# Mixer weights' low halves on GpSimd, merged reciprocals, paired first outputs of the feed-forward stages, and shifted filling, in a two-layer hybrid encoder on one core

## The chip, the cores and the metric

The kernel runs on one core of a Trainium2 chip. The metric is device time in microseconds (us) of one execution. Five engines matter: TensorE (PE; PEld is its weight load, which overlaps PE), VectorE (DVE), ScalarE (ACT), GpSimd (POOL) and SyncE (SP), which here issues the DMAs.

## The reference

```python
for layer in range(DEPTH):                       # DEPTH = 2, D_MODEL = 1024, SEQ = 512
    xn = rms_norm(h, norm_mix_g[layer])
    if layer % 2 == 0:
        mix = even_mixer(...)   # A: top-128 sparse attention by an indexer, 8 heads; B: chunked attention with a bias, 8 heads
    else:
        mix = odd_mixer(...)    # C: forgetting attention, 8 heads; D: sliding window with sinks, 8 query and 2 key heads
    h = h + mix
    h = h + conv_gated_ffn(rms_norm(h, norm_ffn_g[layer]), ...)
return rms_norm(h, norm_out_g)

def conv_gated_ffn(x, w_up, conv_w, conv_b, w_down):      # D_FF = 2816
    g, u = jnp.split(causal_conv3(x @ w_up) + conv_b, 2, axis=-1)
    return (jax.nn.silu(g) * u) @ w_down
```

In A, the indexer's scores are summed over 4 heads, and each query keeps its 128 best admissible keys. Each mixer has an input projection, two groups of heads and an output projection. All numbers are float32.

## The kernel before, in words

**Products.** A float32 product is made of three matmuls on halves: an operand is split into a high half (`hi`, rounded to the matmul's format) and a low half (`lo = x - hi`), and `mm3` (lines 176 to 178) issues hi*hi, hi*lo and lo*hi into one PSUM tile. A step of the filling (below) is one such triple of 512 columns.

**Weights.** All weights stream through the class `Stream` in the fixed order `PLAN`, in tiles of 512 KB: SP loads `raw` (2 buffers), ACT makes `whi` (line 136), and line 138 makes `wlo` by a subtraction. The engine of that subtraction is DVE, and POOL for the keys `A1` and `kB` alone (8 tiles). Keys name the stage: `i` and `d` are small projections, `vB`, `qB`, `kB`, `A1`, `vA`, `A2`, `oA`, `oB` belong to layer 0's mixer, `vC`, `qC`, `kC`, `qD`, `oC`, `oD` to layer 1's, and `g`, `u`, `w` to the feed-forward stages.

**Stages.** Layer 0 runs its indexer and its top-k, B, A and the output projection; then come the feed-forward stage, layer 1 with C, D and its projection, and the second feed-forward stage. Two heads make a `Pair`. Its scores go to PSUM, `soft` (lines 436 to 443) makes a softmax for the four row blocks 1, 2, 0, 3 of 256, 384, 128 and 512 columns: a fused add and minimum on DVE (L439), exp with a sum on ACT (L441), a reciprocal on DVE (L442), a scaling on POOL (L443). `turn` transposes P on PE (L453) and splits it by `PTh` (ACT, L183) and `PTl` (DVE, L184); `av` (L470, L471) multiplies by V; `store` writes Y, and with the pair's second head splits it into `yT`.

**Filling.** `weave` puts the softmax of one pair between the turns of the pair before, and in the gaps has PE do steps of other projections: `fill.step`. How many steps each pair's round gets stands in `FILL_B`, `FILL_A`, `FILL_C` and `FILL_D` (lines 77 to 80). Results of a projection leave PSUM by L546 (`os`, DVE), L547 (`qk` high, ACT) and L548 (`qk` low, POOL). PSUM has 2 buffers `acc`, 4 `s` and 2 `tp`.

**Top-k.** For A, three row blocks of width 256, 384 and 512 (tiles `wk_491`, `wk_545` and `wk_611` in the lists of instructions) each go through 16 rounds of MAX8 (L664) and MATCH_REPLACE8 (L665) on DVE, while B runs.

**Order.** The order of instructions on an engine is made by a scheduler when the program is built; PE stays near program order, while DVE, ACT and POOL are reordered. Each engine then works its own list strictly in that order.

**Other names.** `forget_row` builds for each pair of C a tile `sel` on DVE (L921), with which PE spreads one row of F over 128 partitions (L924). `token_roots` and `roots` make the reciprocal norms of the feed-forward input; `up` runs one chain of a feed-forward product.

Of the kernel before, what the change touches and what calls it, by code (L numbers as in the profile page):

```python
# [10 lines left out]
F32 = mybir.dt.float32  # L11
F32R = mybir.dt.float32r
AF = mybir.ActivationFunctionType
OP = mybir.AluOpType
# [59 lines left out]
WIDE_AT = {k: i for i, k in enumerate(WIDE)}  # L74
NI = 324
ND = 264
FILL_B = (8, 20, 21, 22, 22)
FILL_A = (23, 30, 16, 14, 11)
FILL_C = (6, 18, 16, 15, 12)
FILL_D = (10, 9, 9, 9, 8)  # L80
PARTS = (0, 20, 40, 50, 60, 72, 90, 100)
# [5 lines left out]
def trunk(ctx, tc, a, out):  # L87
# [11 lines left out]
    def bank(tag, shape=(128, 512)):  # L99
        return psum.tile(list(shape), F32, name=tag, tag=tag, bufs=banks[tag])  # L100
# [17 lines left out]
    class Stream:  # L118
# [4 lines left out]
        def issue(self):  # L123
            key = PLAN[self.pos]
            self.pos += 1
            if key[0] == "i":
                src, w = a["w_i"][key[1]], 2 * NI
            elif key[0] == "d":
                src, w = a["w_d"][key[1]], 2 * ND
            else:  # L130
                src, w = a["w"][WIDE_AT[key]], 1024
            raw = wp.tile([128, 1024], F32, name="raw", tag="raw", bufs=2)
            nc.sync.dma_start(raw[:, :w], src)
            hi = wp.tile([128, 1024], F32R, name="whi", tag="whi")
            lo = wp.tile([128, 1024], F32R, name="wlo", tag="wlo")
            nc.scalar.activation(hi[:, :w], raw[:, :w], AF.Copy)  # L136
            eng = nc.gpsimd if key[0] in ('A1', 'kB') else nc.vector
            eng.tensor_tensor(lo[:, :w], raw[:, :w], hi[:, :w].bitcast(F32), OP.subtract)  # L138
            self.ready[key] = (hi, lo)

# [41 lines left out]
    def hilo(dh, dl, src):  # L182
        nc.scalar.activation(dh, src, AF.Copy)  # L183
        nc.vector.tensor_tensor(dl, src, dh.bitcast(F32), OP.subtract)  # L184
# [51 lines left out]
    def token_roots():  # L236
        pt = bank("tp", (128, NT))
        for t in range(NT):
            nc.tensor.matmul(pt[:, t:t + 1], hold_ss["t"][:, t * 128:(t + 1) * 128], ones[:, 0:1],
                             start=True, stop=True)  # L240
        inv_root(rs, pt)

    def roots(t0=0, t1=NT, copy=True):
        n = t1 - t0
        dg = sp.tile([128, NT, 128], F32, name="os", tag="os", bufs=1)
        nc.vector.tensor_tensor(dg[:, :n], ident[:, None, :].to_broadcast([128, n, 128]),
                                rs[:, t0:t1][:, :, None].to_broadcast([128, n, 128]), OP.mult)
        pr = bank("tp", (128, NT, 128))
        nc.tensor.matmul(pr[:, :n], ones, dg[:, :n], start=True, stop=True)
        if copy:  # L250
            nc.scalar.activation(R[:, t0 * 128:t1 * 128].rearrange("p (a d) -> p a d", a=n), pr[:, :n], AF.Copy)
        return pr.rearrange("p a d -> p (a d)")
# [6 lines left out]
    class Fill:  # L259
# [15 lines left out]
        def run(self):  # L275
            while self.q:
                self.step(1)
# [35 lines left out]
    def chan_mm(o, ws, c0=0, c1=SEQ):  # L313
        wh, wl = ws
        for k in range(KD):
            mm3(o[:, c0:c1], wh[:, k, :], wl[:, k, :], xT[0][:, k, c0:c1], xT[1][:, k, c0:c1],
                k == 0, k == KD - 1)
            yield
        later.tick()
# [73 lines left out]
    class Pair:  # L393
# [40 lines left out]
            self.L[e][0], self.L[e][2], self.L[e][3] = P[:, 0:128], P[:, 128:512], P[:, 512:1024]  # L434

        def soft(self, e, rows):
            for i in rows:
                L, nm, sm = self.L[e][i], self.nm[e][:, i:i + 1], self.sm[e][:, i:i + 1]
                nc.vector.tensor_tensor_reduce(out=L, in0=self.s[e][i], in1=self.job["bias"][e][i], scale=1.0,  # L439
                                               scalar=3e38, op0=OP.add, op1=OP.min, accum_out=nm)  # L440
                nc.scalar.activation(L, L, AF.Exp, scale=-1.0, bias=nm, accum_out=sm)  # L441
                nc.vector.reciprocal(sm, sm)  # L442
                nc.gpsimd.tensor_scalar(L, L, sm, 1.0, op0=OP.mult, op1=OP.mult)  # L443

        def turn(self, e, n):
            pk = ([0], [1, 3], [2])[n]
# [26 lines left out]
        def store(self, e):  # L473
            job, o = self.job, self.o[e]
            if e == 0:
                job["Y"] = self.mp.tile([128, 512], F32, name="Y", tag="Y", bufs=self.ybufs)
            Y = job["Y"]
            r = slice(64 * e, 64 * e + 64)
            nc.scalar.activation(Y[r], o[64 * (1 - e):64 * (1 - e) + 64], AF.Copy)
            nc.vector.tensor_tensor(Y[r], o[r], Y[r], OP.add)  # L480
            if e == 1:
                y = job["pair"]["y"] = self.mp.tile([128, 2, 512], F32R, name="yT", tag="yT",
                                                    bufs=5 if self.ybufs == 2 else 4)
                hilo(y[:, 0], y[:, 1], Y)

    def weave(prev, cur, fill, n, mid=None, share=PARTS):
        cut = [n * p // 100 for p in share]
# [264 lines left out]
    def ffn(layer, after):  # L752
        with ExitStack() as st:
            fp = st.enter_context(tc.tile_pool(name=f"ffn{layer}", bufs=1))
            cw = fp.tile([128, 192], F32, name="cw")[:, :4 * NC_FF].rearrange("p (a b) -> p a b", b=4)
            nc.sync.dma_start(cw, a["conv"][layer])
            act = [fp.tile([128, 2, SEQ], F32R, name=f"act{j}") for j in range(NFF)]

            def conv(o, c, dst):
                v = fp.tile([128, SEQ], F32, name="ov", tag="ov", bufs=2)  # L760
                nc.vector.tensor_tensor(v, o, R, OP.mult)  # L761
                nc.scalar.activation(dst, v, AF.Identity, scale=cw[:, c, 2:3], bias=cw[:, c, 3:4])
                nc.vector.scalar_tensor_tensor(dst[:, 1:], v[:, :SEQ - 1], cw[:, c, 1:2], dst[:, 1:],
                                               op0=OP.mult, op1=OP.add)
                nc.vector.scalar_tensor_tensor(dst[:, 2:], v[:, :SEQ - 2], cw[:, c, 0:1], dst[:, 2:],
                                               op0=OP.mult, op1=OP.add)

            def up(key):
                W.ahead(2)
                ws = W.get(key, 128)  # L770
                o = bank("acc" if key[0] == "g" else "s")
                run(chan_mm(o, ws))
                return o

            for j in range(NFF):
                tmp = sp.tile([128, 2, SEQ], F32, name="scr", tag="scr")
                g = up(("g", layer, j))
                if j == 0:
                    token_roots()
                    roots()  # L780
                conv(g, j, tmp[:, 0])
                nc.scalar.activation(tmp[:, 0], tmp[:, 0], AF.Silu)
                u = up(("u", layer, j))
                conv(u, NFF + j, tmp[:, 1])
                nc.vector.tensor_tensor(tmp[:, 0], tmp[:, 0], tmp[:, 1], OP.mult)  # L785
                hilo(act[j][:, 0], act[j][:, 1], tmp[:, 0])
            hold = [None]

            def weights(c, k):
                n = c * NFF + k  # L790
                if n % 8 == 0:
                    W.ahead(2)
                    hold[0] = W.get(("w", layer, n // 8), 128)
                return [x[:, n % 8, :] for x in hold[0]]

            for c in range(KD - 1 if layer else KD):
                o = bank("acc")
                for k in range(NFF):
                    wh, wl = weights(c, k)
                    mm3(o, wh, wl, act[k][:, 0], act[k][:, 1], k == 0, k == NFF - 1)  # L800
                add_resid(c, o)
                after(c, slice(0, SEQ))
            if layer:
                ws = [weights(KD - 1, k) for k in range(NFF)]
                for cols in (slice(0, 256), slice(256, 512)):
                    o = bank("acc")
                    lead_sums(cols)
                    for k in range(NFF):
                        mm3(o[:, cols], *ws[k], act[k][:, 0, cols], act[k][:, 1, cols], k == 0, k == NFF - 1)
                    add_resid(KD - 1, o, cols)  # L810
                    after(KD - 1, cols)
# [33 lines left out]
    with ExitStack() as st:  # L845
# [70 lines left out]

        pairs = [{} for _ in range(4)]

        def forget_row(hh, w):
            sel = mp.tile([128, 128], F32R, name="sel", tag="PSh", bufs=1)  # L920
            nc.vector.tensor_tensor(sel, ident[:, hh:hh + 1].to_broadcast([128, 128]),  # L921
                                    ident[:, 32 + hh:33 + hh].to_broadcast([128, 128]), OP.add)
            pb = bank("s")
            nc.tensor.matmul(pb[:, :w], sel, FTh[:, :w], start=True, stop=True)  # L924
            return pb

        def bias_c(bias, hh, pb, rows):
# [292 lines left out]
```

## Time and profile before

| what | value |
|---|---|
| time, median of 3 runs | 1246.18 us (1245.75 to 1247.45) |
| the profiled execution's own time | 1248.47 us |
| its span, first to last instruction | 1246.6 us |
| mean granted TensorE clock | 0.992 |
| PE busy | 1211.3 us, 97% of the span |
| DVE, ACT, POOL busy | 826.8, 592.6, 198.4 us |

The median is a time of whole executions; the profile is one execution, 2.29 us above that median, of which the span covers all but 1.9 us. Busy shares are means over stages: layer 0's mixer takes the first 300 us or so, its feed-forward stage lasts until about 660 us, layer 1's mixer until about 880 us, and the second feed-forward stage fills the rest.

### The profile page before, as it was taken

The page shows a single profiled execution, that of the slowest core. Times are in us where ns is not written, and L with a number is a line of the kernel's source. Part 1 is how long each engine was busy: PE and PEld are TensorE (multiplying, and loading weights), DVE is VectorE, ACT ScalarE, POOL GpSimd, SP SyncE. Part 2 cuts the span into 40 slices and gives each one's busy share as a digit, 9 for nine tenths or more (in the row PEclk, how much of TensorE's full clock was granted, in tenths as well). Part 3 has the DMA queues.
Part 4 walks back from the last instruction along what each step waited for, and adds up shares of the span by engine and source line. Part 5 has one row for each costly group of instructions (what it writes and reads, how often), then busy time and mean ns, then how long its engine had stood idle before and what let it go on. Part 6 is the DMA issues. An engine that isn't in the chain of part 4 may idle for free.

```text
span 1246.6 us, 15944 instructions
## 1 busy us (share of the span) xinstructions
PE 1211.3 (97%) x5908; PEld 996.3 (80%) x5908; DVE 826.8 (66%) x1528; ACT 592.6 (48%) x1008; POOL 198.4 (16%) x275
## 2 busy tenths in 40 slices
PE   8997999999999999999999999999999999999997
PEld 8776788787888888888888877777888888888886
DVE  7999867867777777742325466897777777772222
ACT  6444465656444444432224577785544444442221
POOL 3465322212000000000002254322000000000000
PEclk9998999999999999999999999999999999999999
DMA  6232124312333333333322321122233233223321
GB/s 215 82 105 68 35 68 135 103 50 88 102 101 96 91 100 102 92 95 101 101 64 90 102 68 35 35 76 75 90 102 98 90 100 102 92 95 101 101 68 68
DMA packets 35373, 111.71 MB, mean 90 GB/s; under 512 B 4192, under 2 KB 6624, under 8 KB 35296
## 3 DMA queue, kind: packets, MB, share of 16 engines
q1 hardware_dynamic: 35296, 110.70, 28.5%
q8 instruction: 46, 0.75, 0.3%
q14 instruction: 31, 0.25, 0.1%
HBM read 108.59 MB, written 2.10 MB: 89 GB/s over the span
## 4 chain that ended last, share of the span: by engine, by line
PE 78%; DVE 11%; ACT 5%; issue 3%; DMA 2%; POOL 1%; POOLq 0%; SPq 0%; DVEq 0%; ACTq 0%
PE acc L176 17%; PE acc L177 17%; PE acc L178 17%; PE s L176 7%; PE s L178 7%; PE s L177 7%; DVE wlo L138 2%; DVE wk L665 2%; DVE m L664 2%; PE tp L453 2%; ACT whi L136 1%; ACT P L441 1%; DMA raw<-in_w 1%; DVE xT L231 1%; DVE P L439 1%
## 5 line engine op out<-in xcount | busy, mean ns | idle before, releaser
L138 DVE TENSOR_TENSOR wlo<-raw,whi 128x1024 fp32r<-128x1024 f32 (+2 forms) x188 | 237.1, 1261 | 158.4 <-ACT whi L136 156.1
L136 ACT ACTIVATE whi<-raw 128x1024 fp32r<-128x1024 f32 (+2 forms) x196 | 204.6, 1044 | 210.8 <-PE acc L177 139.4
L176 PE MATMUL acc<-xT,whi 128*128 128x512 f32 x480 | 189.4, 395 | 1.0 <-DVE os L546 0.6
L178 PE MATMUL acc<-xT,wlo 128*128 128x512 f32 x480 | 187.7, 391 | 0.0
L177 PE MATMUL acc<-xT,whi 128*128 128x512 f32 x480 | 187.7, 391 | 0.0
L213 POOL TENSOR_TENSOR scr<-scr,os 128x512 f32<-128x512 f32 x24 | 34.1, 1421 | 730.5 <-ACT os L211 730.5
L176 PE MATMUL acc<-act,whi 128*128 128x512 f32 (+1 forms) x374 | 140.9, 377 | 0.0
L178 PE MATMUL acc<-act,wlo 128*128 128x512 f32 (+1 forms) x374 | 140.9, 377 | 0.0
L177 PE MATMUL acc<-act,whi 128*128 128x512 f32 (+1 forms) x374 | 140.9, 377 | 0.0
L176 PE MATMUL s<-xT,whi 128*128 128x512 f32 x352 | 137.6, 391 | 0.0
L178 PE MATMUL s<-xT,wlo 128*128 128x512 f32 x352 | 137.5, 391 | 0.0
L177 PE MATMUL s<-xT,whi 128*128 128x512 f32 x352 | 137.0, 389 | 0.0
L176 PEld LDWEIGHTS acc<-xT,whi 128*128 128x128 f32 x480 | 90.7, 189 | 20.9 <-issue 1.9
L178 PEld LDWEIGHTS acc<-xT,wlo 128*128 128x128 f32 x480 | 90.6, 189 | 19.1
L177 PEld LDWEIGHTS acc<-xT,whi 128*128 128x128 f32 x480 | 90.6, 189 | 18.0
L176 PE MATMUL acc<-whi,xT 128*128 128x512 f32 (+2 forms) x208 | 84.1, 406 | 2.1 <-ACT whi L136 1.9
L761 DVE TENSOR_TENSOR ov<-s,R 128x512 f32<-128x512 f32 x44 | 30.4, 692 | 79.6 <-PE s L178 79.6
L183 ACT ACTIVATE act<-scr 128x512 fp32r<-128x512 f32 x44 | 27.8, 631 | 115.8 <-DVE scr L785 115.8
L177 PE MATMUL acc<-wlo,xT 128*128 128x512 f32 (+2 forms) x208 | 80.7, 389 | 1.2 <-DVE wlo L138 1.1
L178 PE MATMUL acc<-whi,xT 128*128 128x512 f32 (+2 forms) x208 | 81.0, 390 | 0.1
L177 PEld LDWEIGHTS acc<-act,whi 128*128 128x128 f32 x374 | 70.4, 188 | 13.0
L178 PEld LDWEIGHTS acc<-act,wlo 128*128 128x128 f32 x374 | 70.4, 188 | 12.9
(250 smaller groups left out, 2235.3 us busy)
## 6 DMA issues: line engine op xcount, KB each, us to landing
raw<-in_w SPq DMA_DIRECT2D x188, 512.0 KB, 3.5
h<-in_x SPq DMA_DIRECT2D x16, 256.0 KB, 4.9
T<-in_relb SPq DMA_DIRECT2D x8, 256.0 KB, 3.0
raw<-in_w_i SPq DMA_DIRECT2D x4, 324.0 KB, 4.1
raw<-in_w_d SPq DMA_DIRECT2D x4, 264.0 KB, 2.7
out_y<-h SPq DMA_DIRECT2D x4, 256.0 KB, 2.2
out_y<-h SPq DMA_DIRECT2D x2, 384.0 KB, 2.4
ropeC<-in_ropeC SPq DMA_DIRECT2D x2, 256.0 KB, 4.0
```

The source lines that it names most:

```text
L136: nc.scalar.activation(hi[:, :w], raw[:, :w], AF.Copy)
L138: eng.tensor_tensor(lo[:, :w], raw[:, :w], hi[:, :w].bitcast(F32), OP.subtract)
L176: nc.tensor.matmul(o, lh, rh, start=start, stop=False)
L177: nc.tensor.matmul(o, lh, rl, start=False, stop=False)
L178: nc.tensor.matmul(o, ll, rh, start=False, stop=stop)
L183: nc.scalar.activation(dh, src, AF.Copy)
L213: eng.tensor_tensor(ss, ss, sq, OP.add)
L231: nc.vector.scalar_tensor_tensor(xT[1][:, c, :], H["h"][:, c, :], g, xT[0][:, c, :].bitcast(F32), op0=OP.mult, op1=OP.subtract)
L453: nc.tensor.transpose(pt[:, off:off + 128], self.L[e][i][:, j * 128:(j + 1) * 128], ident)
L664: nc.vector.max(m8, wk)
L665: nc.vector.match_replace(wk, m8, wk, -3e38)
L761: nc.vector.tensor_tensor(v, o, R, OP.mult)
```

## The change

- `Stream`: `wlo` of all mixers' wide tiles is made on POOL; `i`, `d`, `g`, `u`, `w` stay on DVE. 48 subtractions move (24 in each layer).
- `soft`: the sums of rows 2, 0, 3 lie in adjacent columns and get one reciprocal; the scalings of the three follow it. 96 reciprocals become 48.
- `store`: the low half of `yT` goes from DVE to POOL, for 12 pairs.
- The feed-forward stage begins with `first_two`, which takes the first output of g and the first of u in step (6 of 8 steps of each, then the rest), and only then calls `token_roots` and `roots`.
- `forget_row`: `sel` is gone; PE's weights are a broadcast column of a small tile `pick`, made once.
- `FILL_B` gets 11 steps more, `FILL_A` 11 fewer.

```diff
-FILL_B = (8, 20, 21, 22, 22)
-FILL_A = (23, 30, 16, 14, 11)
+FILL_B = (8, 24, 24, 24, 24)
+FILL_A = (20, 22, 18, 12, 11)
...
-            eng = nc.gpsimd if key[0] in ('A1', 'kB') else nc.vector
+            eng = nc.vector if key[0] in ("i", "d", "g", "u", "w") else nc.gpsimd
             eng.tensor_tensor(lo[:, :w], raw[:, :w], hi[:, :w].bitcast(F32), OP.subtract)
...
         def soft(self, e, rows):
+            at = {1: 3, 2: 0, 0: 1, 3: 2}
+            nms, sms = self.nm[e], self.sm[e]
             for i in rows:
-                L, nm, sm = self.L[e][i], self.nm[e][:, i:i + 1], self.sm[e][:, i:i + 1]
+                L, nm, sm = self.L[e][i], nms[:, at[i]:at[i] + 1], sms[:, at[i]:at[i] + 1]
...
                 nc.scalar.activation(L, L, AF.Exp, scale=-1.0, bias=nm, accum_out=sm)
-                nc.vector.reciprocal(sm, sm)
-                nc.gpsimd.tensor_scalar(L, L, sm, 1.0, op0=OP.mult, op1=OP.mult)
+            both = sms[:, at[rows[0]]:at[rows[-1]] + 1]
+            nc.vector.reciprocal(both, both)
+            for i in rows:
+                L = self.L[e][i]
+                nc.gpsimd.tensor_scalar(L, L, sms[:, at[i]:at[i] + 1], 1.0, op0=OP.mult, op1=OP.mult)
...
-                hilo(y[:, 0], y[:, 1], Y)
+                nc.scalar.activation(y[:, 0], Y, AF.Copy)
+                nc.gpsimd.tensor_tensor(y[:, 1], Y, y[:, 0].bitcast(F32), OP.subtract)
...
+            def first_two():
+                W.ahead(2)
+                os_ = bank("acc"), bank("s")
+                gens = [chan_mm(o, W.get((x, layer, 0), 128)) for x, o in zip("gu", os_)]
+                for gen in gens:
+                    for _ in range(KD - 2):
+                        next(gen)
+                for gen in gens:
+                    run(gen)
+                return os_
...
-                g = up(("g", layer, j))
                 if j == 0:
+                    g, u = first_two()
                     token_roots()
                     roots()
+                else:
+                    g = up(("g", layer, j))
...
-                u = up(("u", layer, j))
+                if j > 0:
+                    u = up(("u", layer, j))
...
+        pick = mp.tile([128, 32], F32R, name="pick")[:, :8]
+        nc.vector.tensor_tensor(pick, ident[:, 0:8], ident[:, 32:40], OP.add)
...
         def forget_row(hh, w):
-            sel = mp.tile([128, 128], F32R, name="sel", tag="PSh", bufs=1)
-            nc.vector.tensor_tensor(sel, ident[:, hh:hh + 1].to_broadcast([128, 128]),
-                                    ident[:, 32 + hh:33 + hh].to_broadcast([128, 128]), OP.add)
             pb = bank("s")
-            nc.tensor.matmul(pb[:, :w], sel, FTh[:, :w], start=True, stop=True)
+            nc.tensor.matmul(pb[:, :w], pick[:, hh:hh + 1].to_broadcast([128, 128]), FTh[:, :w],
+                             start=True, stop=True)
             return pb
```

In the changed kernel some lines have other numbers: L664 to L666 are L670 to L672, L546 is L552, L548 is L554, L439 is L441, L443 is L448, L1064 is L1085.

**DVE in B, at the first `PTl` (the low half of the first transposed P).** In the kernel before, DVE's list there, with the top-k's rounds on `wk_545` and `wk_611` and the projection's exit `os`, reads:

```order
L546 SCALAR_TENSOR_TENSOR os<-acc,R 128x512
L664 MAX m_1793<-wk_545 128x8
L665 MATCH_REPLACE wk_545<-m_1793,wk_545 128x384
L664 MAX m_1796<-wk_545 128x8
L665 MATCH_REPLACE wk_545<-m_1796,wk_545 128x384
L664 MAX m_1799<-wk_545 128x8
L664 MAX m_1804<-wk_611 128x8
L184 TENSOR_TENSOR PTl<-tp,PTh 128x512
```

In the changed kernel the list up to the same `PTl` reads:

```order
L552 SCALAR_TENSOR_TENSOR os<-acc,R 128x512
L670 MAX m_1827<-wk_611 128x8
L671 MATCH_REPLACE wk_611<-m_1827,wk_611 128x512
L670 MAX m_1830<-wk_611 128x8
L671 MATCH_REPLACE wk_611<-m_1830,wk_611 128x512
L670 MAX m_1833<-wk_611 128x8
L671 MATCH_REPLACE wk_611<-m_1833,wk_611 128x512
L670 MAX m_1836<-wk_611 128x8
L552 SCALAR_TENSOR_TENSOR os<-acc,R 128x512
L671 MATCH_REPLACE wk_611<-m_1836,wk_611 128x512
L184 TENSOR_TENSOR PTl<-tp,PTh 128x512
```

The third top-k block has begun earlier against `PTl`, and one more `os` stands ahead of it. Up to the fifth `PTl`, DVE's list before holds 8 `wlo` of B's weights and 10 of the 16 rounds of `wk_611`; the changed one holds no such `wlo` and all 16 rounds, with 2 rope products (L341) more, one `yT` and 8 reciprocals fewer, and the threshold of `wk_611` besides.

**POOL at the start of layer 0.** One piece of the difference, from the squares of x (L224) through the bias tiles `T`, the rope tables and the indexer's rope additions (L343):

```order
 L224 TENSOR_TENSOR scr<-scr 128x1024 x2
-L673 TENSOR_SCALAR T<-T 128x512
-L674 MEMSET T 64x64
-L673 TENSOR_SCALAR T<-T 128x512
-L674 MEMSET T 64x64
-L257 TENSOR_SCALAR ropeC<-ropeC,rs 128x128
+L138 TENSOR_TENSOR wlo<-raw,whi 128x1024
+L679 TENSOR_SCALAR T<-T 128x512
+L138 TENSOR_TENSOR wlo<-raw,whi 128x1024
```

The first `wlo` of `vB` now stand on POOL among the indexer's preparations; the third and fourth follow between the rope tables and additions, the fourth behind two L343.

**POOL in D.** The list before, with the scalings of D's P (L1064) and the rope additions of D's queries (L343):

```order
L1064 TENSOR_SCALAR P<-P,sm 128x128 x3
L343 TENSOR_TENSOR scr_7155<-scr 128x512
L1064 TENSOR_SCALAR P<-P,sm 128x128 x3
L1064 TENSOR_SCALAR PP<-PP,sm 128x256 x5
L343 TENSOR_TENSOR scr_7325<-scr 128x512
L1064 TENSOR_SCALAR PP<-PP,sm 128x256
```

The changed list at the same place:

```order
L343 TENSOR_TENSOR scr_7085<-scr 128x512
L138 TENSOR_TENSOR wlo<-raw,whi 128x1024 x2
L1085 TENSOR_SCALAR P<-P,sm 128x128 x3
L490 TENSOR_TENSOR yT<-Y,yT 128x512
L1085 TENSOR_SCALAR PP<-PP,sm 128x256 x5
L343 TENSOR_TENSOR scr_7255<-scr 128x512
L1085 TENSOR_SCALAR PP<-PP,sm 128x256
L138 TENSOR_TENSOR wlo<-raw,whi 128x1024 x3
```

Runs of two and three `wlo`, and the low half of a `yT`, now stand between the scalings.

## Rows read from the trace of the kernel before

**Rows 1.** The page's first part: busy time, share of the span, instructions of each engine.

```profile
PE 1211.3 (97%) x5908; PEld 996.3 (80%) x5908; DVE 826.8 (66%) x1528; ACT 592.6 (48%) x1008; POOL 198.4 (16%) x275
```

**Rows 2.** Length, PE, PEld, DVE, ACT, POOL busy us (instructions), PE's clock, DMA, by stretch.

```profile
20.00:140.00 120.00, 109.03 (x554) 86.38 (x552) 114.80 (x315) 56.78 (x117) 60.35 (x74) 0.97 0.29 91
97.30:104.15 6.85, 6.00 (x18) 4.92 (x19) 6.78 (x21) 1.80 (x5) 1.07 (x3) 0.50 0.01 2
140.00:280.00 140.00, 136.11 (x762) 111.18 (x761) 101.84 (x254) 81.00 (x180) 34.37 (x52) 1.00 0.26 82
320.00:660.00 340.00, 340.00 (x1517) 282.19 (x1517) 201.62 (x246) 131.62 (x161) 9.65 (x8) 1.00 0.31 95
660.00:780.00 120.00, 117.34 (x641) 94.87 (x640) 73.12 (x195) 74.67 (x160) 43.42 (x82) 1.00 0.24 72
780.00:860.00 80.00, 77.13 (x467) 61.80 (x466) 67.44 (x195) 57.78 (x153) 19.78 (x34) 1.00 0.17 54
```

**Rows 3.** What PE waited for from 60 to 140 us: total, times, longest.

```profile
PE tp L420 <- DVE PTl L184: 6.9, 2, 4.9
PE tp L420 <- ACT qk L547: 1.1, 1, 1.1
PE tp L420 <- POOL qk L548: 0.9, 1, 0.9
PE tp L470 <- DVE PTl L184: 0.7, 1, 0.7
```

**Rows 4.** The timeline from 88 us: start, duration, instruction, [idle before, and its releaser].

```profile
93.26 0.68 DVE L546 SCALAR_TENSOR_TENSOR os<-acc,R 128x512 f32<-128x512 f32 x1
...
94.51 0.58 ACT L183 ACTIVATE PTh<-tp 128x512 fp32r<-128x512 f32 x1
...
97.42 0.67 DVE L184 TENSOR_TENSOR PTl<-tp,PTh 128x512 fp32r<-128x512 f32 x1
...
98.15 0.58 PE L420 MATMUL tp<-qk 64*128 64x256 f32 x1 [4.90 <-DVE PTl L184]
```

**Rows 5.** DVE's groups by shape, 20 to 140 us: busy us, mean ns, idle before.

```profile
L664 DVE MAX8 m<-wk 128x8 f32<-128x512 f32 x16 | 11.1, 691 | 0.3
L665 DVE MATCH_REPLACE8 wk<-m,wk 128x512 f32<-128x512 f32 x16 | 10.8, 675 | 0.0
...
L665 DVE MATCH_VALUE_LOAD wk<-m,wk 128x8 f32 x48 | 4.1, 86 | 0.9
...
L442 DVE RECIPROCAL sm<-sm 128x1 f32<-128x1 f32 x21 | 3.2, 156 | 0.3 <-ACT P L441 0.2
...
L341 DVE TENSOR_TENSOR scr<-acc,ropeS 128x256 f32<-128x256 f32 x2 | 0.7, 410 | 0.0
```

**Rows 6.** Line 138 (`wlo`): minimum, median and maximum ns, first and last start.

```profile
L138 DVE TENSOR_TENSOR wlo<-raw,whi x188: 698/1225/3021, 7.2 to 1212.6; 128x1024 fp32r<-128x1024 f32 x180, 128x648 fp32r<-128x648 f32 x4, 128x528 fp32r<-128x528 f32 x4
...
L138 POOL TENSOR_TENSOR wlo<-raw,whi x8: 2372/2404/2980, 52.5 to 121.5; 128x1024 fp32r<-128x1024 f32 x8
```

**Rows 7.** The timeline of DVE, 58 to 63.5 us.

```profile
59.55 0.74 DVE L647 SCALAR_TENSOR_TENSOR wk<-P,wi,wk 128x512 f32<-128x512 f32 x1
...
60.55 2.62 DVE L647 SCALAR_TENSOR_TENSOR wk<-P,wi,wk 128x512 f32<-128x512 f32 x1
```

**Rows 8.** The timeline of POOL, 30 to 66 us.

```profile
60.22 2.40 POOL L138 TENSOR_TENSOR wlo<-raw,whi 128x1024 fp32r<-128x1024 f32 x1 [4.72 <-ACT whi L136]
```

**Rows 9.** The tile `yT`: its split on DVE, minimum, median, maximum ns.

```profile
L184 DVE TENSOR_TENSOR yT<-Y,yT x12: 680/692/2050, 122.4 to 802.7; 128x512 fp32r<-128x512 f32 x12
```

**Rows 10.** Line 548, a POOL subtraction of the same shape as `yT`: minimum, median, maximum.

```profile
L548 POOL TENSOR_TENSOR qk<-os,qk x16: 1267/1305/1880, 66.9 to 760.2; 128x512 fp32r<-128x512 f32 x16
```

**Rows 11.** What PE waited for from 140 to 310 us.

```profile
PE acc L176 <- DVE h L346: 1.7, 1, 1.7
...
PE acc L177 <- DVE wlo L138: 0.7, 1, 0.7
```

**Rows 12.** What PE waited for from 660 to 880 us.

```profile
PE s L924 <- DVE sel L921: 0.5, 3, 0.2
```

## The prediction

> **What bounds the kernel now.** I read the busy shares first, then the busy time by stretch, PE's waits in each stretch, and around the longest wait the timeline. PE is busy 97% of the span, DVE 66%, POOL 16% [rows 1]. So nothing can be won but PE's idle time, and a removed instruction of another engine is worth only the PE wait that it ends. In the feed-forward stretch PE is busy for all of 340 us with 1517 matmuls, 0.224 us each [rows 2]; nothing that DVE or POOL does there counts. The rows of a stretch then give the idle time to be won: 10.97 us in B (120 - 109.03), 3.89 in A, 2.66 in C, 2.87 in D [rows 2]. In B, DVE is busy for 114.80 of 120 us, and B is the one place where PE waits because DVE's list is full: 6.9 us in two waits for `PTl`, 2.0 for the projection's exit (`qk` high and low), 0.7 for another `PTl` [rows 3]. The longest wait, until 98.15, reads as follows: `os` runs at 93.26, because top-k rounds stand ahead of it; ACT, which works in order and has `qk` to take from it, comes to `PTh` only at 94.51; DVE comes to `PTl` at 97.42; PE starts at 98.15 [rows 4]. Right behind that idle time the granted clock is 0.50 (1.2 GHz) from 97.30 to 104.15, where it is 1.00 (2.4 GHz) before and after [rows 2]; half of 6.85 us, 3.4, is lost by it. In D, DVE is busy for 67.44 of 80 us; in A and C it is at 73% and 61%.
>
> **The change part by part.** The sum is made against the profiled execution, 1248.47 us, 2.29 above the median of 1246.18; a difference carries over to the median unchanged.
>
> *Filling, in B.* 11 steps of three matmuls more: 33 x 0.224 = 7.4 us of PE work go from A to B. In B they lie in gaps in which PE waits for DVE, and there are 10.97 us of such idle time, so all of it can be hidden. Bounds: 0 (if the gaps are elsewhere) and 7.4. I take **7.4**, because FILL_B's rounds are where the waits of [rows 3] stand.
>
> *DVE's list in B.* The wait until 125 us is for the fifth `PTl` of DVE's list, so I count what stands ahead of that one, before and after (the count behind the first pair of lists above). Out: 8 `wlo` of 1.225 [rows 6] = 9.8; 8 reciprocals net of 0.156 [rows 5] = 1.2; one `yT` of 0.69 [rows 9]. In: 6 rounds of top-k, each 0.691 + 0.675 + 0.086 = 1.45 [rows 5], = 8.7; two rope products and a threshold, at least 0.41 each [rows 5], 1.5 taken. Net -1.5: the scheduler spends nearly all of the freed time on earlier top-k rounds, which are worth nothing before `PTl`. I take **1.5** (0 to 11, the upper end if the waits are for the exits `os`, which lose their `wlo` ahead and gain fewer rounds).
>
> *What POOL's subtractions do to DVE, in B.* POOL needs 2.404 us for what DVE does in 1.225 [rows 6]. Worse, while POOL runs its `wlo` from 60.22 to 62.62 [rows 8], DVE's L647, with two inputs in SBUF, takes 2.62 instead of the 0.74 of the same shape just before [rows 7]: 1.88 us lost. A `yT` split took 2.05 at most against a median of 0.692 [rows 9]: 1.36. These two are the clear hits among the 8 `wlo` that POOL makes now, 3.24 / 8 = 0.4 us for each. Eight more come into B (`vB`, `qB`). The four of `vB` stand among the indexer's preparations, which are rich in such two-input work (second list above), so I double the price there: 4 x 0.4 + 4 x 0.8 = **-4.8**. Bounds: 8 x 0.4 = 3.2, and 8 x 1.88 = 15.0 if each hits.
> The Trainium skill (GPSIMD Engine Reference, section 1) says that GpSimd's SBUF interface is shared with VectorE, with contention for instructions with two SBUF inputs; the rows on L647 agree. Taken strictly, any overlap of the two kinds costs, which is the upper bound, and the first rival. The same page, section 4.1, advises VectorE for two-input elementwise work, GpSimd being about twice as slow; the trace has 2.404 / 1.225 = 1.96.
>
> *Clock.* If the wait of 4.90 us shrinks, so may the 3.4 lost behind it. Bounds 0 and 3.4; nothing in the trace says how short the idle time must become, so half: **1.7**.
>
> *A.* PE waits 0.7 for a `wlo` already [rows 11], with the tile made on DVE; on POOL it is ready 2.404 - 1.225 = 1.18 later wherever it is made just in time. `vA` and `A2` have eight such tiles; the four projections' tiles after them have time. I take one tile just in time of each kind, 0.9 and 1.1. The last pair's `yT` low half costs 1.305 (as L548 [rows 10]) against 0.692 [rows 9], 0.6 later, and A's end waits for that chain. Against this, 16 `wlo` leave DVE (19.6 us of 101.84); of A's 3.89 idle I credit 1.6. Net **-1.0**, bounds -9 (all eight tiles late) and +3.9. The 1.7 at L346 [rows 11] stays: its DVE work is the same.
>
> *C.* `sel` ends a wait of 0.5 [rows 12]: +0.5. Its 12 builds otherwise lie beside PE work. The three scalings of P now wait for the last exp, and 12 `wlo` join POOL (43.42 of 120 us busy, so 72 after). One `wlo` of `vC` just in time takes 0.5. Net **0**, bounds -6 (12 x 0.5) and +2.6.
>
> *D.* Eight to nine `wlo` (about 10 us) leave a DVE that is busy for 67.44 of 80 us; POOL goes from 19.78 to about 40. The third pair of lists shows runs of two and three `wlo`, 4.8 to 7.2 us, between scalings. I take half of the idle time of 2.87: **+1.5**, bounds -4 and +2.9.
>
> *At nothing.* `first_two`: PE has no idle time once the feed-forward stretch runs, and the same matmuls are done; without that cover the roots' transposes would cost a fraction of a us. The reciprocals outside B: hidden, 0.156 each.
>
> Sum: 7.4 + 1.5 - 4.8 + 1.7 - 1.0 + 0 + 1.5 = **6.3 us faster**: 1248.47 - 6.3 = 1242.2 for such an execution, 1246.18 - 6.3 = **1239.9** for the median.
>
> **The rivals.**
> 1. *Contention eats B.* Every one of the eight new POOL subtractions in B stretches a DVE instruction by 1.88. For: DVE has no slack there (114.80 of 120), and the `vB` tiles stand beside two-input work. Against: MAX8, MATCH_REPLACE8 and everything read from PSUM make up most of DVE's time, and the MAX8 beside that `wlo` was not stretched. 15.0 in place of 4.8: 1239.9 + 10.2 = 1250.1.
> 2. *GpSimd's queue, the slower side.* Outside B's `vB` and `qB`, 40 `wlo` stand in POOL's list ahead of scalings of P and of `qk` low, 2.4 us each and up to three in a row. If the instruction behind is delayed so that PE waits 0.3 us on average for each, that is 12 us: 1251.9. It decides from 6.3 / 40 = 0.16 us each. For: POOL's list is in order and the scalings are on the way to PE's transposes. Against: POOL stays under two thirds busy, and the filling covers most delays.
> 3. *A gives back what B wins (no change).* A loses 11 steps of cover; if its softmax rounds then wait 7.4 us longer, the sum is +1.1: 1247.3. For: A is now idle for just 3.89 of 140 us with that cover. Against: A's DVE is at 73% and loses 16 `wlo`.
> 4. *All of B's waits go.* B's idle time of 10.97 and the clock's 3.4 come back nearly whole, and 2.5 in D, with A's 1.0 lost: -16, 1230. For: the `os` exits gain up to 5 us on DVE's list by the same count.
>
> **How the numbers follow.** The forecast, with everything from 1233 to 1243.7, has 0.42; the fourth rival (below 1233) 0.20; the third, or parts that cancel (1243.7 to 1248.7), 0.20; the first 0.08 and the second 0.10. 0.2% is 2.5 us, about what a measurement can tell from no change. So faster 0.62, same 0.20, slower 0.18. The range from 1229 to 1250 leaves out about half of the slow rivals and a part of the fourth; the forecast's own range is 1233 to 1244.
>
> **What would show it.** Filling: more than 554 instructions on PE from 20 to 140 us, and PE's waits for `PTl` there at 3 us or less in all, in place of 7.6. Clock: the stretch at 0.50 shorter or gone. Contention: some DVE instructions of two SBUF inputs at 1.5 to 2.6 us where a POOL `wlo` lies beside them, from 20 to 80 us. A: waits for `wlo` on POOL of about 2 us in all. C: none for `sel`. D: PE busy for over 78 of its 80 us. Feed-forward stretches unchanged. It is wrong if PE waits long for scalings of P or `wlo` by POOL (second rival), if A's idle time grows beyond 7 us (third), or if B's early stretch gains several us on DVE by stretched instructions (first).

## The result and the profile after

The changed kernel takes 1276.47 us (median of 4 runs, 1276.31 to 1276.9) against 1246.78 for the kernel before beside it: the ratio is 1.0239, interval 1.0222 to 1.0257. It is slower by about 30 us, where 6.3 us faster was forecast. The profiled execution took 1276.43 us, with a span of 1274.7, 28.1 above that of before.

Busy time from the page of the changed kernel, first part:

```profile
PE 1216.8 (95%) x5908; PEld 1002.7 (79%) x5908; DVE 769.8 (60%) x1409; ACT 590.9 (46%) x1008; POOL 314.7 (25%) x335
```

DVE lost 57 us and POOL gained 116. PE has the same 5908 matmuls and is busy 5.5 us longer, though nothing was added to it; its idle time within the span grew by 22.6 us, from 35.3 to 57.9. Busy time by stretch, columns as in [rows 2]:

```profile
20.00:140.00 120.00, 103.48 (x509) 82.16 (x508) 108.25 (x279) 51.39 (x103) 72.24 (x76) 0.93 0.28 88
140.00:280.00 140.00, 129.04 (x714) 106.83 (x713) 72.68 (x211) 76.95 (x177) 75.57 (x77) 0.96 0.25 76
320.00:660.00 340.00, 340.00 (x1504) 281.26 (x1503) 207.33 (x255) 137.43 (x167) 7.21 (x5) 1.00 0.30 96
660.00:780.00 120.00, 115.19 (x614) 96.06 (x613) 40.87 (x123) 62.54 (x126) 68.55 (x78) 0.99 0.25 80
780.00:860.00 80.00, 74.66 (x446) 58.60 (x444) 58.73 (x185) 59.85 (x167) 43.80 (x61) 0.98 0.13 40
```

Against [rows 2], PE's idle time has grown in every stretch of the mixers: 10.97 to 16.52 us in the first, 3.89 to 10.96 in the second, 2.66 to 4.81 and 2.87 to 5.34 in C's and D's; the feed-forward stretch is as full as before. (The stretches are fixed in time, while the changed kernel comes to its later stages up to 28 us later, so they no longer hold quite the same work.) DVE has much more room, 72.68 us busy of 140 in A where it was 101.84, and that bought nothing. The clock column adds to it: 0.93 and 0.96 in the mixer of layer 0, where it was 0.97 and 1.00. The same view of the eight stretches in which the granted clock is 0.50 (the first, the third, the fifth and the sum):

```profile
38.23:45.05 6.82, 5.87 (x14) 4.62 (x15) 4.10 (x10) 0.69 (x1) 2.65 (x5) 0.50 0.23 77
...
109.91:116.73 6.82, 4.32 (x14) 3.61 (x15) 6.69 (x18) 2.43 (x6) 2.72 (x3) 0.50 0.29 103
...
243.03:249.85 6.82, 4.65 (x15) 3.98 (x16) 2.04 (x4) 1.25 (x3) 4.44 (x3) 0.50 0.51 161
...
sum 37.55, PE 31.13 PEld 25.97 DVE 21.22 ACT 9.99 POOL 19.89; mean PE 3.89 PEld 3.25 DVE 2.65 ACT 1.25 POOL 2.49
```

Besides the kernel's tail, these come to 37.55 us; the kernel before has three, with this sum:

```profile
sum 13.68, PE 12.83 PEld 10.98 DVE 12.78 ACT 8.53 POOL 2.97; mean PE 4.28 PEld 3.66 DVE 4.26 ACT 2.84 POOL 0.99
```

At 1.2 in place of 2.4 GHz half of the time in which PE works there is lost, 15.6 us after and 6.4 before (PE's idle time in them is waiting, and is not counted). So some 9 us of the 28.1 are clock, as an estimate, and some 19 are waits; by the first part of the page it would be 5.5 of busy and 22.6 of idle time.

PE's waits in three stretches (from 20, 140 and 660 us), the longest totals of each: total, times, longest; first 20 to 140 us:

```profile
PE acc L177 <- POOL wlo L138: 5.5, 2, 3.8
PE tp L420 <- DVE PTl L184: 5.1, 2, 4.5
PE acc L176 <- DVE os L552: 2.8, 1, 2.8
...
```

140 to 310 us:

```profile
PE tp L704 <- POOL scr L343: 6.2, 1, 6.2
PE acc L177 <- POOL yT L490: 2.5, 2, 2.1
...
```

660 to 880 us:

```profile
PE acc L176 <- DVE h L346: 4.0, 2, 2.4
PE tp L420 <- POOL qk L554: 2.2, 1, 2.2
PE acc L176 <- DVE sm L1077: 1.3, 1, 1.3
...
```

Where [rows 3, 11, 12] name DVE in five of seven lines, POOL now stands in four of these eight lines. Three places show how.

**The list of POOL in A.** The timeline of POOL from 231 us:

```profile
236.94 1.61 POOL L448 TENSOR_SCALAR P<-P,sm 128x384 f32<-128x384 f32 x3
240.37 2.35 POOL L138 TENSOR_TENSOR wlo<-raw,whi 128x1024 fp32r<-128x1024 f32 x1 [1.82 <-ACT whi L136]
242.67 1.26 POOL L490 TENSOR_TENSOR yT<-Y,yT 128x512 fp32r<-128x512 f32 x1
243.89 1.26 POOL L343 TENSOR_TENSOR scr<-scr 128x512 f32<-128x512 f32 x1
```

and PE's next matmul:

```profile
245.20 1.12 PE L704 MATMUL tp<-ident,scr 128*128 128x128 f32 x4 [6.24 <-POOL scr L343]
```

DVE had made the rope products for that L343 by 238.04, and POOL was free from 238.55. But its next instruction is a `wlo` whose `whi` comes only at 240.3, and then the low half of `yT`: L343 starts 5.3 us after it could. PE waits 6.24 us; the stretch at 0.50 from 243.03 begins within that wait.

**DVE's two-column sums in D.** The timeline of DVE from 842 us:

```profile
842.23 0.15 DVE L1075 TENSOR_TENSOR es<-nm,sink 128x2 f32<-128x2 f32 x1
...
843.40 2.36 DVE L1075 TENSOR_TENSOR es<-nm,sink 128x2 f32<-128x2 f32 x1
845.68 0.47 DVE L1067 CUSTOM_DVE_ANT_0 P<-s,dmask,nsink 128x256 f32<-128x256 f32 x1
...
847.25 0.68 DVE L346 TENSOR_TENSOR h<-acc,h 128x512 f32<-128x512 f32 x1
```

POOL and PE there:

```profile
843.33 2.41 POOL L138 TENSOR_TENSOR wlo<-raw,whi 128x1024 fp32r<-128x1024 f32 x1 [5.26 <-ACT es L1076]
```

```profile
847.99 0.50 PE L176 MATMUL acc<-yT,whi 128*128 128x512 f32 x1 [1.59 <-DVE h L346]
```

A sum of two columns takes 0.15 us, and 2.36 when it starts beside a `wlo`: it ends at 845.76, 0.02 us after POOL's instruction. DVE works in order, so what stands behind it, among it the `h` for which PE waits to have an `acc` buffer free, can be up to 2.2 us late by it.

**The `vB` tiles.** POOL, DVE and PE from 30 us:

```profile
30.88 2.36 POOL L138 TENSOR_TENSOR wlo<-raw,whi 128x1024 fp32r<-128x1024 f32 x1
...
36.74 2.38 POOL L138 TENSOR_TENSOR wlo<-raw,whi 128x1024 fp32r<-128x1024 f32 x1
```

```profile
31.02 2.58 DVE L341 TENSOR_TENSOR scr<-ir,ropeC 128x320 f32<-128x320 f32 x1
...
37.03 2.44 DVE L341 TENSOR_TENSOR scr<-ir,ropeC 128x320 f32<-128x320 f32 x1
```

```profile
39.18 0.80 PE L177 MATMUL acc<-wlo,xT 128*128 128x512 f32 x1 [3.77 <-POOL wlo L138]
```

The last two tiles are late for PE by 1.7 and 3.8 us, the fourth because it stands behind seven small instructions of the indexer, among them two L343. DVE finishes a rope product for the second of these 2 us late, because it is held beside the third tile. The stretch at 0.50 from 38.23 begins 0.95 us before the longer wait ends.

### The profile page after: what moved, and what is told of

Same layout as the page of the kernel before. It is cut to its first block, busy times and chain, and to the rows that moved or that the text cites. A ratio compares the mean times of both kernels' runs of the same rounds, so it can differ in the third digit from the quotient of the medians.

```text
span 1274.7 us, 15919 instructions
## 1 busy us (share of the span) xinstructions
PE 1216.8 (95%) x5908; PEld 1002.7 (79%) x5908; DVE 769.8 (60%) x1409; ACT 590.9 (46%) x1008; POOL 314.7 (25%) x335
## 4 chain that ended last, share of the span: by engine, by line
PE 72%; DVE 10%; POOL 6%; issue 5%; ACT 4%; DMA 2%; POOLq 0%; SPq 0%; DVEq 0%; ACTq 0%
PE acc L177 15%; PE acc L178 15%; PE acc L176 15%; PE s L178 7%; PE s L177 7%; PE s L176 7%; POOL wlo L138 3%; DMA raw<-in_w 2%; DVE wk L671 2%; DVE m L670 2%; PE tp L458 1%; ACT whi L136 1%; PE tp L475 1%; PE tp L476 1%; DVE PTl L184 1%
## 5 line engine op out<-in xcount | busy, mean ns | idle before, releaser
L138 DVE TENSOR_TENSOR wlo<-raw,whi 128x1024 fp32r<-128x1024 f32 (+2 forms) x140 | 172.6, 1233 | 144.0 <-ACT whi L136 141.3
L138 POOL TENSOR_TENSOR wlo<-raw,whi 128x1024 fp32r<-128x1024 f32 x56 | 134.7, 2410 | 63.5 <-ACT whi L136 49.0
L176 PE MATMUL acc<-whi,xT 128*128 128x512 f32 (+2 forms) x208 | 85.5, 411 | 1.4 <-ACT whi L136 1.2
L178 PE MATMUL acc<-whi,xT 128*128 128x512 f32 (+2 forms) x208 | 82.4, 396 | 1.3 <-DVE xT L231 1.3
L177 PEld LDWEIGHTS acc<-act,whi 128*128 128x128 f32 x374 | 70.4, 188 | 13.0
L176 PEld LDWEIGHTS acc<-act,whi 128*128 128x128 f32 x374 | 70.3, 188 | 12.8
```

The costliest lines, as they stand in the source:

```text
L176: nc.tensor.matmul(o, lh, rh, start=start, stop=False)
L177: nc.tensor.matmul(o, lh, rl, start=False, stop=False)
L178: nc.tensor.matmul(o, ll, rh, start=False, stop=stop)
```

## The experiments

Diffs are against the changed kernel, unless another is named. Times are medians; ratios are to the kernel before. Without the moved low halves of the weights the changed kernel takes 1246.3 us (first run), and losses are counted from there. The kernel before was run again beside each group of runs, and its median lay between 1245.67 and 1246.94 us, so differences of about 1 us between runs of different groups mean little.

**All but the weights' low halves.**

```diff
-            eng = nc.vector if key[0] in ("i", "d", "g", "u", "w") else nc.gpsimd
+            eng = nc.gpsimd if key[0] in ('A1', 'kB') else nc.vector
```

> All of the change but the 48 low halves of the weights, which go back to DVE. Theory 1 (GpSimd's list: the subtractions of 2.4 us stand in its list between work that TensorE waits for, and each wait of some us is followed by a stretch at half the clock): nearly all of the 30 us goes, 1240 to 1250 us. Theory 2 (the shifted filling or the later scalings are at fault): at least half of the loss stays, 1260 us or more. Theory 3 (the low half of yT on GpSimd is at fault): it stays as well, above 1260 us.

1246.27 us, ratio 0.9998 (0.9988 to 1.0008).

**The weights' low halves alone**: that line, the other way round, in the kernel before.

> The kernel before with the 48 low halves moved to GpSimd and nothing else. Theory 1: 1268 to 1280 us. Theories 2 and 3: 1242 to 1252 us.

1279.64 us, ratio 1.0267 (1.0251 to 1.0282). These two put the whole loss, some 30 us, on the 48 subtractions, which by themselves cost 33; the rest of the change is worth nothing on balance without them, and some 3 us beside them.

**`yT` on DVE**: line 490's subtraction on `nc.vector`.

> All of the change but the low half of yT, which goes back to DVE. The profile after has 2.5 us of TensorE waiting for that tile, and it stands ahead of the rope addition for which TensorE waited 6.2 us. Theory 1: 3 to 9 us come back, 1267 to 1273 us. Theory 3: more than 15 us come back, below 1261 us. Theory 2: no change.

1275.12 us, 1.4 less than the change: theory 3 falls, and theory 1's figure too. The wait for L343 is gone from the trace, but one of 3.5 us for L341's rope products stands in its place.

**The old filling**: `FILL_B` and `FILL_A` as before.

> All of the change but the shifted filling, which goes back to its old numbers. Theory 1: within 5 us of the change, 1271 to 1281 us, and slower if the shift is worth what was predicted (+7). Theory 2: at least 10 us come back, below 1266 us.

1274.4 us, 2.1 less: theory 2 falls, and the shift is worth nothing here.

**Only layer 1's low halves moved.**

```diff
+            eng = nc.gpsimd if key[0] in ('A1', 'kB', 'vC', 'qC', 'kC', 'qD', 'oC', 'oD') else nc.vector
```

> All of the change, but the 24 low halves of layer 0 that moved go back to DVE; layer 1's 24 stay on GpSimd. The profile after puts 20.6 us of the delay before the first feed-forward stage's second half and 7 in layer 1. If the loss is a sum over places, 1252 to 1258 us. If only layer 0's tight list matters and layer 1 follows from it, 1244 to 1249 us.

1259.12 us, ratio 1.0103 (1.0082 to 1.0124). The loss adds up over places: 17.4 us in layer 0 (1276.5 - 1259.1) and 12.9 in layer 1 (1259.1 - 1246.3), more of it in layer 1 than the trace's delays had suggested.

**`vB` on DVE**: "vB" among the keys of `nc.vector`.

> All of the change, but the four vB tiles go back to DVE. In the profile after, TensorE waits 5.5 us for two of them, with a stretch at half the clock behind (3.4 us lost). Theory of single late tiles: 6 to 12 us come back, 1264 to 1270 us. Rival (DVE's list, full from there on, takes the time back): 3 us or less come back, 1273 us or more.

1267.66 us: `vB` costs 8.8 us.

**`oB` on DVE**, likewise.

> All of the change, but the four oB tiles go back to DVE. In the profile after, TensorE waits 6.2 us for a rope addition of GpSimd that stands in its list behind a subtraction of an oB tile and the low half of a yT, and runs at half the clock for 6.8 us behind it. Theory Q (GpSimd works its list in order): 5 to 9 us come back, 1267 to 1271 us. If the wait only moves on, 1273 us or more.

1271.42 us: 5.1 us back, 0.4 short of theory Q's range. PE's wait at that place, 140 to 320 us:

```profile
PE tp L704 <- POOL scr L343: 2.5, 1, 2.5
```

Of 6.2 us 2.5 stay: L343 starts behind the `yT` half, at 238.62, and then takes 2.25 us in place of 1.26, beside a `wlo` that DVE now makes from 237.56 to 239.75.

**Only C's and `qD`'s low halves moved** (as for layer 1, without `oC` and `oD`).

> As the run with only layer 1's low halves on GpSimd (1259.1 us), but oC and oD go back to DVE, so that in D only qD's stand on GpSimd. Theory L: the holds of 1.6 to 2.4 us of the sinks' two-column sums in D go, and with them TensorE's waits of 6.4 us there and a stretch or two at half the clock, 1248 to 1253 us. Theory Q puts the loss in C (the low half of qk behind the subtractions): 1256 to 1260 us.

1250.24 us, ratio 1.0038 (1.0025 to 1.0051): `oC` and `oD` in D cost 8.9 us, the remaining 16 tiles of layer 1 4.0. Theory L's forecast holds, theory Q's does not, and none of the two-column sums is held in the trace.

**The sinks' sums on ScalarE, with layer 1's low halves on GpSimd.**

```diff
-                    nc.vector.tensor_tensor(es, self.nm[g][:, c], sink[:, 4 * g + 2 * u:4 * g + 2 * u + 2], OP.add)
-                    nc.scalar.activation(es, es, AF.Exp)
-                    nc.vector.tensor_tensor(sm, sm, es, OP.add)
+                    for j in range(2 * u, 2 * u + 2):
+                        es1, sm1 = self.es[g][:, j:j + 1], self.sm[g][:, j:j + 1]
+                        nc.scalar.activation(es1, self.nm[g][:, j:j + 1], AF.Exp, bias=sink[:, 4 * g + j:4 * g + j + 1])
+                        nc.scalar.activation(sm1, es1, AF.Identity, bias=sm1)
```

> As the run with only layer 1's low halves on GpSimd (1259.1 us), but the sinks' two-column sums in D are made on ScalarE, with a bias, and no longer on DVE with two inputs in SBUF; GpSimd's work is the same. Theory L (those sums wait until GpSimd's subtraction is over): most of the 8.9 us goes that the oC and oD tiles cost, 1249 to 1254 us. Theory Q (GpSimd's list): 1257 to 1262 us.

1250.08 us (1247.34 to 1253.79). Its control, the same sums with the weights' low halves on DVE:

> The control for it: all of the change with the weights' low halves on DVE (1246.3 us), and the same sums on ScalarE. By all theories within 3 us of 1246.3; what it differs is the price of the sums' move itself.

1249.45 us (1245.56 to 1252.21): the move of the sums by itself costs 3.2 us, just outside the 3 expected. With these sums the 24 tiles of layer 1 cost 0.6 us in place of 12.9, though POOL does the same work; both medians spread over 6 us, so nothing and 3 can't be told apart, but 13 is excluded. (The 4.0 us of C and `qD`, which these sums don't touch, should have stayed; that they don't show in the 0.6 says that they are uncertain too.) The stretch from 780 to 860 us, with layer 1's tiles on GpSimd and the sums on DVE:

```profile
780.00:860.00 80.00, 71.87 (x406) 55.85 (x405) 60.08 (x180) 54.72 (x150) 36.79 (x46) 0.96 0.15 47
```

and with the sums on ScalarE:

```profile
780.00:860.00 80.00, 77.53 (x468) 60.98 (x468) 55.39 (x155) 66.77 (x203) 38.70 (x44) 1.00 0.17 54
```

62 more matmuls in the same 80 us, at full clock, with POOL as busy: D is theory L. It also says that taking 24 subtractions from DVE in layer 1 is worth nothing, once they do no harm.

**Four pieces.** Each moved subtraction in pieces of 256 columns.

> All of the change, with each of the 48 moved subtractions made in four pieces of 256 columns on GpSimd. In the profile after, DVE instructions with two inputs in SBUF that meet one of these subtractions end their own length after it ended, even one of two columns, which took 2.36 us. Theory L (such an instruction waits until GpSimd's instruction at hand is over): the longest hold falls from 2.4 to about 0.7 us, and 8 to 18 us come back, 1258 to 1268 us. Theory Q (GpSimd's list and its whole time): the time on GpSimd is the same or a little more, 1274 to 1286 us.

1268.67 us, 7.8 back, just short of theory L's range. From the tile's list, one piece (minimum, median, maximum ns):

```profile
L140 POOL TENSOR_TENSOR wlo<-raw,whi x192: 713/735/1197, 21.8 to 872.1; 128x256 fp32r<-128x256 f32 x192
```

Four pieces take 2.94 us in place of 2.40, and yet it is faster, so the length of one instruction counts beside the whole time; the two-column sums in its trace take 0.71 us at most, in place of 2.36. PE's wait for the rope addition in A is 6.5 us there: a list in order isn't mended by pieces.

**Copies.** These leave the subtraction out: raw copied once; raw twice; `whi` and then raw.

> Leaves out the subtraction of the 48 moved low halves: GpSimd copies raw instead, with one input from SBUF, once, in about half the time. Theory 1a (GpSimd's list and its time): half to two thirds of the loss goes, 1255 to 1262 us. Theory 1b (two SBUF inputs at once hold up DVE's instructions): more than three quarters goes, 1246 to 1253 us.

> Leaves out the subtraction as in the run with the copy, but makes the copy twice, so that GpSimd is held for about as long as by a subtraction (some 2.4 us a tile), with one input from SBUF. Theory 1a (GpSimd's list and its time): the loss stays, 1268 to 1280 us. Theory 1b (two SBUF inputs at once hold up DVE's instructions): most of it goes, 1246 to 1257 us.

> Leaves out the subtraction: GpSimd copies whi and then raw into the same tile, two instructions of about 1.05 us with one input, which wait for ScalarE's whi as the subtraction does (the run with two copies of raw did not). Theory L, shorter instructions on GpSimd: the same as with two copies of raw, 1249 to 1257 us. Theory D (that run gained because it no longer waited for ScalarE): 1262 to 1276 us.

1238.4, 1252.62 and 1252.29 us; the first is below both ranges. In the last, the two instructions:

```profile
L140 POOL TENSOR_SCALAR wlo<-whi x48: 1033/1050/1944, 20.6 to 852.6; 128x1024 fp32r<-128x1024 f32 x48
L140 POOL TENSOR_SCALAR wlo<-raw x48: 1036/1050/1362, 22.6 to 853.7; 128x1024 fp32r<-128x1024 f32 x48
```

Waiting for `whi` makes no difference, so theory D falls. Two instructions of 1.05 us cost 6 us where one of 2.40 costs 30, and one of 1.05 gains 8. That is not theory 1b as it was put: in the trace with two copies of raw, two-column sums beside a copy also end with it, after 0.3 to 1.1 us. A single input on GpSimd's side doesn't free DVE; the hold is only shorter. The scheduler makes other lists for each of these kernels, so how the 24 us split between shorter holds and shorter queues isn't settled by them. Nor is the gain of the single copy explained; PE is busier behind B, 174.67 of the 180 us from 140 in place of 171.35 in the first run.

**The rest alone.** Reciprocals, feed-forward beginning and `pick`; both low halves and the filling as before.

> The kernel before with the merged reciprocals, the feed-forward stages' beginning and the column in place of sel, without the moved low halves (weights and yT) and with the old filling. If the shifted filling gives back in A what it wins in B, this is as good as the run with all but the weights' low halves or better, 1241 to 1246 us. If the filling is worth what was forecast (7 us), this is worse than it, 1247 to 1253 us.

1244.56 us, ratio 0.9988 (0.9978 to 0.9997): the one version with all of its work that is faster than the kernel before, by about 0.1%.

**That, with `qB` on GpSimd.**

> The best so far (merged reciprocals, the feed-forward beginning and the column, 1244.6 us), with the four qB tiles alone on GpSimd. Their neighbours on DVE are mostly top-k rounds, which the subtraction does not hold up, and they are ready long before TensorE needs them. Theory L: faster, 1239 to 1243 us. Theory Q (any subtraction in the list costs, with the projection's low halves behind it): 1246 to 1251 us.

1247.15 us, ratio 1.0003 (0.9989 to 1.0016): worse than without by 2.6 us (1.9 by the ratios), in theory Q's range. But its trace shows theory L's mechanism. DVE's L652, which adds up the indexer's scores from two inputs in SBUF and takes 0.74 us, meets two subtractions one behind the other (POOL from 58.62 to 63.83):

```profile
59.27 2.29 DVE L652 SCALAR_TENSOR_TENSOR wk<-P,wi,wk 128x512 f32<-128x512 f32 x1
...
61.83 2.54 DVE L652 SCALAR_TENSOR_TENSOR wk<-P,wi,wk 128x512 f32<-128x512 f32 x1
```

PE's wait from 40 to 140 us for the exit that DVE makes behind them is

```profile
PE acc L176 <- DVE os L551: 3.8, 2, 2.5
```

in place of 1.0, 1, 1.0 without, and the 0.9 us that PE waited there for the projection's low half on POOL is gone. What was wrong was the expectation that the neighbours are mostly top-k rounds: two that are not were enough.

## Why the prediction was wrong

**The step that failed is the price of a moved subtraction.** I charged B for eight tiles with 4.8 us, credited D with 1.5, put C at 0 and A at -1.0. Measured by undoing: `vB` -8.8, the rest of layer 0, by difference, -8.5 (of it `oB` -5.1), C with `qD` -4.0, `oC` and `oD` -8.9; together the 30 us, each to about 1 us.

- **D** was wrong in sign. I took half of PE's idle time as won because DVE was relieved, and priced contention only for B's large instructions. The two-column sums are 0.15 us long and were in none of my rows; they are held for up to 2.2 us and have the whole of DVE's list behind them.
- **The hits in B** were mis-sized. L647's 2.62 us [rows 7] was read as a slowdown by 1.88; it is a wait for the end of POOL's instruction, and any such instruction with two inputs in SBUF can suffer it. The Trainium skill (SBUF — State Buffer, "SBUF: two separate sides") says it so: the port pair that GpSimd shares with VectorE is locked for a whole instruction, and the loser blocks. The trace agrees, with 843.40 + 2.36 against 843.33 + 2.41. It also allows for the reverse, GpSimd held by VectorE; the trace agrees, with a `wlo` of 3.10 us from 20.52 in place of 2.40, beside DVE's L224, which has two inputs and runs until 21.37. In the changed kernel L653 (the old L647) is held twice in B, for 1.7 and 1.8 us, and the wait of 2.8 us for `os` comes behind it.
- **`vB`** I priced by contention alone. That the fourth tile stands behind two L343 I had shown in the list and given no price; it is 3.8 us of waiting and some 2.9 of clock (half of the 5.87 us in which PE works from 38.23 to 45.05).
- **A**: the second rival's mechanism (GpSimd's list in order) is what stands before 245 us, where I had written that the tiles after `vA` and `A2` "have time". They do; what stands behind them in the list hasn't.
- **Clock**, +1.7 forecast: some -9. I gave a bonus for a wait that might shrink and no price to the waits that might come. The 3.4 us that I read off the stretch before was a little too much as well: it begins 0.85 us before PE's wait ends, PE works for 6.00 of its 6.85 us, and half of that is 3.0.
- **Filling**, +7.4 forecast: nothing. Without the moved tiles, PE is busy for 112.37 us of B's 120 with the new filling (first run) and for 111.45 with the old one (the rest alone, where `yT`'s low half is on DVE too), and for 171.35 and 174.49 of the 180 behind it. So B wins at most 1 us, and A gives back 3, as the third rival had it. That all 7.4 us can be hidden in B was wrong: PE runs 567 instructions there with the 11 steps more and 570 without. The old filling is 2.1 us better in the changed kernel.
- **DVE's relief**, +1.5: not seen in B. In the changed kernel PE still waits 4.5 us for a `PTl` in B, which the new list puts behind four rounds on `wk_611` and an `os`.
- **Right**: nothing happens in the feed-forward stretches; `sel`'s wait is gone; `first_two` and the reciprocals outside B are worth about nothing (with `sel`, 1.1 us in all). The second rival had the direction, with 0.10, and 25 us too little; it left out the holds and the clock. The first rival, with 0.08, had the holds, but in B alone.

In D the cause is shown, by the sums' move and its control. Left open: what the hold and the queue take each in `vB` and in the rest of layer 0, where both occur at the same tiles.

## What to carry to other kernels

Before moving work to GpSimd, list every VectorE instruction with two inputs in SBUF that can fall beside it, the tiny ones too, and price each at up to GpSimd's whole instruction plus what is queued behind it. Then read GpSimd's new list for instructions that TensorE waits for behind a long one that waits itself. Relieving an engine that isn't the bound promises little: VectorE lost 57 us of work here, and the kernel 30 us of time; even the single copy, with the subtraction left out, gained 8.

## What the runs showed of the hardware

- In the changed kernel thirteen `TENSOR_TENSOR` and `SCALAR_TENSOR_TENSOR` of VectorE with both inputs in SBUF start while GpSimd makes a `wlo`. All thirteen end 0.02 to 0.56 us after it: that is their own length, less at most 0.2 us, so 0.02 us for two columns (0.15 alone) and 0.55 for 512 (0.69 or 0.74 alone). Top-k rounds, instructions that read PSUM, and reciprocals that start there keep their usual length (MAX8 of 512 columns 0.68 to 0.70 us).
- All eight stretches at 1.2 GHz in the changed kernel, 3.4 or 6.8 us long, begin within a wait of PE of 1.7 to 6.2 us or at most 2.1 us after one of 0.9 to 2.1 us. Half of PE's 31.13 us in them, 15.6 us, is what they cost; behind the 6.24 us at L343 it is 2.3 of 4.65. Not every wait has one: behind those of 2.80 us until 77.63 and of 2.43 until 862.68 the granted clock stays at 1.00 for 8 us and more.
